# Halved operands for the output product, second pair's weights formed earlier, and the entry's low parts on VectorE, in one hybrid decoder layer

## The chip, the cores and the metric

The kernel runs on 1 core of one Trainium2 chip. The metric is the device time of one launch in microseconds (us), the median of several runs. All times below are in us unless ns is written. Engines are called as the profile calls them: PE (TensorE, matrix products), ACT (ScalarE), DVE (VectorE), POOL (GpSimd), SP (SyncE, which issues every DMA of this kernel).

## What is computed

One layer (DEPTH is 1) of a decoder with parallel branches, for 1024 prompt positions and 8 x 4 sample positions with the same weights. The kernel puts both side by side: 1056 columns of tokens, features on the 128 partitions.

```
h = RMSNorm(x);  p = h @ w_in
A = retention -> GroupNorm -> swish gate;  B = spatial gating unit;  C = cross-attention
x = x + (sig(gA)*A@w_br_ret + sig(gB)*B@w_br_sg + sig(gC)*C@w_br_x) @ w_o      # D = 1024
z = RMSNorm(x) @ w_up                                                          # 2 x 2816 columns
zc = conv_b + sum(conv_w[j] * z shifted by j)                                  # causal, width 3
a, b = split(zc);  x = x + (gelu(a) * b) @ w_down;  y = RMSNorm_final(x)
```

The change touches the second half of this: the product with w_o ("wo" in the code), the norm behind it, the first two of the 22 pairs of columns of w_up, and the entry of the product with w_down.

## The kernel before

**Every fp32 product is three products.** An operand is split into a high part (ACT copies it into the type fp32r) and a low part (value minus high part, one subtraction on DVE or POOL). PE then adds high*high, high*low and low*high in PSUM. So a product needs two elementwise instructions ahead of it for each operand, weights too. `split` makes both parts, `x_split` makes the high part and, if it is given an engine (`vtt` is DVE, `ptt` is POOL), the low part; `x_low` makes a low part alone.

**Order.** The whole kernel is a schedule written out by hand: each engine runs its instructions in the order of the program. Work that belongs beside a product is put in one of two ways: generators in `gens`, of which `hook()` takes a step after every k step of a product at a rate that is set for each stage; and the list `todo` (L1486), of which `do()` takes one entry after every k step of the first products of w_up. An entry's place in the list sets the order in the queues, not a time: an engine runs ahead until something it needs is missing.

**Buffers.** `slot` gives one of 40 buffers of 128 x 1056 (NSLOT); an instruction that writes a new tile waits until the buffer's last reader is done. Weights pass through two raw buffers (`wr`) and three pairs of split buffers (`wh`, `wl`). PSUM holds two accumulators of three banks (`mp`) up to w_o and three of two banks (`bp`) in the products with w_up.

**The stages around the change.** First the branch product "br" (m = 0..7): `mops` gets, for each m, the high and low part of the merged branches over all 1056 columns, the low part on POOL. Then the product with w_o, in two token halves of 528 columns (`half`), each m = 0..7 with eight k steps of six matmuls; behind each m DVE adds the product to the residual (`x2c`), ACT squares, DVE sums the squares, and the half is written to DRAM (`scx`). Beside the second half runs `half_norm` (L1260): the norm of the first half (`norm_sums`, `norm_root`), then for each k the scaling on DVE (`h_scale`, L1257) and the split into the operands B11 and B21, low parts on POOL.

**The first pair of w_up** (the "entry", L1507) is a plain product: two rows r (columns j and 22 + j) times two token halves, each a sum of s = 0, 1. Beside it `todo` norms and scales the second half (A), forms its low parts (L) into B12 and B22, and then the sums and differences t1 to t4 and the splits T2, T3, T1, T4.

**The other 21 pairs** use a 2 x 2 scheme with seven products in place of eight: B11, B21, B22, T2, T3, T1, T4 each times one block of the weights or a sum of blocks. `f_dma` loads a pair's raw weights, `f_sums` forms s1 to s4, `f_prep0` to `f_prep3` split a11|a12, s2|s3, s1|s4 and a22. The products' results are put together with additions that read PSUM (`put`, `put_t`, `z_put`), mostly on DVE. Beside pair j DVE runs the convolution of pair j - 1 (`Conv.first` on ACT, `tap` twice for each of a and b on DVE, `gelu` on ACT, `conv_end` on DVE). Pair 1 is written out (L1539 to 1572), pairs 2 to 21 are the loop at L1593.

**The entry of w_down** is prepared in the last pair by `first_down` (L1574), five steps: loads and splits of the first activations (`a_load`, `a_split`) and weights (`w_dma`, `w_prep`), and the loads of the residual (`x2_load`, eight DMAs from `scx` into `x2t`) in its fourth and fifth step. In `down` DVE adds each finished product to `x2t[m]`; `last_conv` runs beside it.

## Time and profile before

| | us |
|---|---|
| median of 3 runs | 1964.17 (1964.1 to 1965.32) |
| the profiled execution: its time | 1969.01 |
| the profiled execution: its span | 1967.2 |
| PE busy in the span | 1885.8 (96%) |
| DVE, POOL, ACT busy | 1071.7, 963.2, 615.6 |
| mean granted TensorE clock | 0.984 of full speed |
| product "br" ends, product with w_o ends | 1100.5, 1197.9 |
| entry, pair 1, pair 2, pairs 3 to 21 begin | 1199.0, 1230.2, 1260.9, 1291.2 |
| product with w_down begins | 1679.7 |

The last three rows are the starts of matmuls in the timeline of PE, counted from the start of the span. "Busy" is the share of time in which an instruction was under way on an engine; a matmul's end is modelled and matmuls overlap, so the count of matmuls in a stretch says more than the busy time. A row of the chain of waits names an engine, a line of the kernel, and what released it. Nearly all subtractions and sums have L112 (DVE), L115 (POOL) or L118 (DVE, with a scalar), and all matmuls L106, since helpers record them; the tiles' names tell them apart: `mgl` is a low part of `mops`, `xh`/`xl` are the parts of B11 to T4, `wh`/`wl`, `fh`/`fl`, `f` and `fs` are split weights and their sums, `x2c` the residual and the scaled rows, `t` the buffers of t2, `ns`/`nst` the norm, `c` the convolution, `zt`/`zu`/`z`/`zs` results put together, `x` the tiles of `x2t`.

### The profile page before, as it was taken

To read this page: it belongs to the slowest core of one execution; us is meant where nothing else is said; L and a number is where in the kernel's file an instruction comes from. 1 tells how busy PE (TensorE), PEld (TensorE's weight loads), DVE (VectorE), ACT (ScalarE), POOL (GpSimd) and SP (SyncE) were. 2 spreads that over 40 slices of the span, in tenths; PEclk is the share of its full clock that TensorE was granted. 3 is DMA by queue.
4 is the path that set the end of the run, shared out by engine and by line. 5 is a ranking of instruction groups with operands and counts; after the bars stand their busy time and mean duration, and the time that the engine had idled before them with its cause. 6 is when DMAs were issued, how large, how long until landed. Compare 5 with 4: busy or idle time off the path is not lost.

```text
span 1967.2 us, 31365 instructions
## 1 busy us (share of the span) xinstructions
PE 1885.8 (96%) x13201; PEld 1856.8 (94%) x13201; DVE 1071.7 (54%) x1480; ACT 615.6 (31%) x954; POOL 963.2 (49%) x594
## 2 busy tenths in 40 slices
PE   6999999999989999999999999899999999899997
PEld 6999998999989999999999998799999999799996
DVE  8463636453464531111112266699999999644446
ACT  5232232322224332111131233534434344321204
POOL 6242433231644424334254456777777777653404
PEclk9999999999999999999999999899999999899998
DMA  4112131324133313111221532122222223632202
GB/s 182 54 44 90 44 102 37 127 65 152 54 131 108 98 30 146 42 45 48 88 93 43 184 130 76 44 66 88 76 79 77 74 88 99 251 124 105 75 1 89
DMA packets 51740, 174.50 MB, mean 89 GB/s; under 512 B 5712, under 2 KB 8944, under 8 KB 51600
## 3 DMA queue, kind: packets, MB, share of 16 engines
q1 hardware_dynamic: 51600, 172.50, 26.3%
q8 instruction: 104, 1.70, 0.3%
q14 instruction: 36, 0.29, 0.1%
HBM read 137.04 MB, written 35.43 MB: 88 GB/s over the span
## 4 chain that ended last, share of the span: by engine, by line
PE 77%; DVE 9%; issue 5%; ACT 3%; POOL 3%; DMA 2%; SPq 0%; DVEq 0%; POOLq 0%; ACTq 0%
PE mp L106 53%; PE bp L106 19%; PE ap L106 4%; DVE c L118 1%; POOL wl L115 1%; POOL mgl L115 1%; DVE hl L118 1%; DVE s L112 1%; ACT sw L476 1%; DMA xr<-in_xT 1%; DVE x2c L118 1%; DMA scr<-ox 0%; POOL xl L115 0%; DVE rt L118 0%; DVE st L526 0%
## 5 line engine op out<-in xcount | busy, mean ns | idle before, releaser
L115 POOL TENSOR_TENSOR wl<-wr,wh 128x1024 fp32r<-128x1024 f32 x115 | 296.5, 2581 | 425.5 <-ACT wh L150 378.4
L106 PE MATMUL mp<-hh,wh 128*128 128x384 f32 (+1 forms) x1152 | 263.6, 337 | 10.2 <-ACT hh L109 5.3
L106 PE MATMUL mp<-hl,wh 128*128 128x384 f32 (+1 forms) x1152 | 253.8, 328 | 5.0 <-DVE hl L118 5.0
L106 PE MATMUL mp<-hh,wl 128*128 128x384 f32 (+1 forms) x1152 | 251.1, 325 | 0.0
L106 PE MATMUL bp<-xl,wh 128*128 128x264 f32 (+2 forms) x1056 | 217.3, 288 | 6.1 <-POOL xl L115 5.7
L106 PE MATMUL bp<-xh,wh 128*128 128x264 f32 (+2 forms) x1056 | 216.5, 286 | 6.1 <-DVE zu L112 3.5
L106 PE MATMUL bp<-xh,wl 128*128 128x264 f32 (+2 forms) x1056 | 216.3, 286 | 2.1 <-POOL wl L115 2.1
L106 PEld LDWEIGHTS mp<-hh,wh 128*128 128x128 f32 x1152 | 192.2, 191 | 13.2 <-ACT hh L109 5.5
L106 PEld LDWEIGHTS mp<-hl,wh 128*128 128x128 f32 x1152 | 193.3, 190 | 7.5 <-DVE hl L118 7.5
L106 PEld LDWEIGHTS mp<-hh,wl 128*128 128x128 f32 x1152 | 193.3, 190 | 0.0
L112 DVE TENSOR_TENSOR x<-x,mp 128x288 f32<-128x288 f32 (+3 forms) x167 | 105.7, 675 | 128.1 <-PE mp L106 119.2
L106 PEld LDWEIGHTS bp<-xl,wh 128*128 128x128 f32 x1056 | 166.6, 191 | 8.3 <-POOL xl L115 7.3
L106 PEld LDWEIGHTS bp<-xh,wh 128*128 128x128 f32 x1056 | 166.7, 191 | 7.2 <-issue 5.1
L106 PEld LDWEIGHTS bp<-xh,wl 128*128 128x128 f32 x1056 | 166.8, 191 | 2.5 <-POOL wl L115 2.5
L115 POOL TENSOR_TENSOR wl<-fs,wh 128x1024 fp32r<-128x1024 f32 x41 | 123.8, 3020 | 51.4 <-ACT wh L1285 51.3
L118 DVE SCALAR_TENSOR_TENSOR c<-z,hist,c 128x1024 f32<-128x1024 f32 x88 | 134.2, 1526 | 17.8 <-ACT c L109 17.8
L106 PE MATMUL mp<-ach,whs 128*128 128x384 f32 (+3 forms) x524 | 125.1, 328 | 9.2 <-DVE x L112 8.3
L150 ACT CAST wh<-wr 128x1024 fp32r<-128x1024 f32 x100 | 103.9, 1041 | 75.6 <-PE mp L106 50.0
L106 PE MATMUL mp<-acl,whs 128*128 128x384 f32 (+3 forms) x524 | 124.9, 328 | 0.0
L106 PE MATMUL mp<-ach,wls 128*128 128x384 f32 (+3 forms) x524 | 124.8, 328 | 0.0
L112 DVE TENSOR_TENSOR th<-mp,rst 128x768 f32<-128x768 f32 (+1 forms) x48 | 31.7, 701 | 170.9 <-PE mp L106 150.3
L118 DVE SCALAR_TENSOR_TENSOR th<-th,mp 128x768 f32<-128x768 f32 (+1 forms) x48 | 31.7, 701 | 145.4 <-PE mp L106 145.4
(352 smaller groups left out, 4132.7 us busy)
## 6 DMA issues: line engine op xcount, KB each, us to landing
wr<-in_wslab SPq DMA_DIRECT2D x164, 512.0 KB, 3.6
sca<-c SPq DMA_DIRECT2D x22, 528.0 KB, 3.0
opr<-sca SPq DMA_DIRECT2D x22, 528.0 KB, 4.5
opr<-scr SPq DMA_DIRECT2D x16, 528.0 KB, 5.4
scr<-ort SPq DMA_DIRECT2D x8, 528.0 KB, 7.6
x2c<-in_xT SPq DMA_DIRECT2D x8, 528.0 KB, 7.6
scx<-x2c SPq DMA_DIRECT2D x16, 264.0 KB, 2.9
x<-scx SPq DMA_DIRECT2D x8, 528.0 KB, 9.6
```

The source lines that it names most:

```text
L106: nc.tensor.matmul(out=out, lhsT=l, rhs=r, start=start, stop=stop)
L112: nc.vector.tensor_tensor(out=out, in0=a, in1=b, op=op)
L115: nc.gpsimd.tensor_tensor(out=out, in0=a, in1=b, op=op)
L118: nc.vector.scalar_tensor_tensor(out=out, in0=a, scalar=s, in1=b, op0=op0, op1=op1)
L150: nc.scalar.copy(out=hi, in_=raw)
L476: nc.scalar.copy(out=o[a:a + 64], in_=i[b:b + 64])
```

## The change

Five edits in one function.

1. `mops` holds, for each half of the tokens, a list of eight tiles with the high part in the first 528 columns and the low part in the next 528. ACT and POOL run two instructions of 528 columns for each m in place of one of 1056. The product with w_o reads the tiles of its half.
2. The second pair's raw weights (`raw1`) are loaded into buffers of their own behind m = 5 of the first half; a11|a12, the four sums (all on DVE), a22 and s2|s3 are formed in `early1` behind m = 1, 2, 4 and 5 of the second half. s1|s4 and the loads of pair 2 come at the second entry of `todo`. Pair 2's weights are formed earlier in pair 1: a11|a12 behind its first product, the sums behind its third, all on POOL, s2|s3 behind the fourth, s1|s4 behind the fifth.
3. Low parts: in `half_norm` on DVE, one k behind the high part; all eight L, and T1, T3 and T4, on DVE (before: four L on DVE and four on POOL; T1, T3, T4 on POOL). The list `todo` is written anew.
4. In the entry's second half both rows use an operand before the next: (s 0, row 0), (s 0, row 1), (s 1, row 0), (s 1, row 1).
5. `x2_load` moves from the fourth and fifth step of `first_down` to the first and second.

```diff
                 gens.append(late())
             tha.append(gate(("ga", m), 0, m))
         drain()
-        mops = []
+        mops = [[], []]
         for m in range(8):
             ps = fm(("br", m), aops)
             gated(tha[m], ps)
             vtt(acc[m], acc[m], tha[m], ALU.add)
-            mops.append(split(acc[m], "mg"))
+
+            for half in range(2):
+                t = slot("mg", F32R)
+                src = acc[m][:, half * HW:(half + 1) * HW]
+                nc.scalar.copy(out=t[:, 0:HW], in_=src)
+                ptt(t[:, HW:2 * HW], src, f(t)[:, 0:HW], ALU.subtract)
+                mops[half].append(t)
 
 
         x2c = []
...
 
         def half_norm():
 
+            low = lambda k: x_low(("B11", "B21")[k // 4], k % 4, hs(k, 0), vtt)
             norm_sums(0)
             yield
             norm_root(0)
             for k in range(8):
                 h_scale(k, 0)
-                x_split(("B11", "B21")[k // 4], k % 4, hs(k, 0), ptt)
+                x_split(("B11", "B21")[k // 4], k % 4, hs(k, 0), None)
+                if k:
+                    low(k - 1)
                 yield
+            low(7)
 
 
         fraw, fw = {}, {}
...
 
         fsum = {}
 
-        def f_sums(j, sub):
+        def f_sums(j, sub, sub34=ptt):
 
             a11, a12, a21, a22 = f_quads(j)
             fsum[j] = (slot("fs"), slot("fs"))
             s2, s3, s1, s4 = [t[:, 512 * i:512 * i + 512] for t in fsum[j] for i in range(2)]
             sub(s1, a21, a22, ALU.add)
             sub(s2, s1, a11, ALU.subtract)
-            return lambda: (ptt(s3, a11, a21, ALU.subtract), ptt(s4, a12, s2, ALU.subtract))
-
-        def f_prep0(j):
+            return lambda: (sub34(s3, a11, a21, ALU.subtract), sub34(s4, a12, s2, ALU.subtract))
+
+        def f_prep0(j, own=False):
             fw[j] = {}
-            f_parts(j, ("a11", "a12"), fraw[j][0])
+            f_parts(j, ("a11", "a12"), fraw[j][0], own)
 
         def f_prep1(j, own=False):
             f_parts(j, ("s2", "s3"), fsum[j][0][:, 0:1024], own)
...
             ptt(t[:, 512:1024], a22, f(t)[:, 0:512], ALU.subtract)
             fw[j]["a22"] = (t[:, 0:512], t[:, 512:1024])
             del fraw[j]
-            f_dma(j + 1)
+            if j > 1:
+                f_dma(j + 1)
+
+
+        def raw1():
+            fraw[1] = [slot("fr", shape=[P, 1024]) for _ in range(2)]
+            for t, key in zip(fraw[1], (("up", 1), ("up", NFF + 1))):
+                dma(t, wslab[SLABS.index(key)])
+
+        early1 = [int, lambda: f_prep0(1, True), lambda: f_sums(1, vtt, vtt)(), int, lambda: f_prep3(1),
+                  lambda: f_prep1(1, True), int, int]
 
         for half in range(2):
             rate[0] = 0.25
...
                 lv = lo.rearrange("p (k c) -> p k c", c=P)
                 ps = mp()
                 for k in range(8):
-                    rh, rl = mops[k]
+                    rh, rl = mops[half][k][:, 0:HW], mops[half][k][:, HW:2 * HW]
                     for i, (a, r) in enumerate(((hv, rh), (hv, rl), (lv, rh))):
                         for q in range(2):
-                            c0 = half * HW + q * QW
+                            c0 = q * QW
                             mm(ps[:, q, 0:QW], a[:, k, :], r[:, c0:c0 + QW], start=(k == 0 and i == 0),
                                stop=(k == 7 and i == 2))
                     if k == 0 or k == 3:
                         w_ahead()
-                        if wst["p"] == FAST0 and 1 not in fraw:
-                            f_dma(1)
                     hook()
                 w_free(key)
                 o = quarters(hs(m, half))
...
                     act(sq[:, 0:HW], hs(m, half), AF.Square)
                     vtt(s, s, sq[:, 0:HW], ALU.add)
                 dma(scx[m][:, half * HW:(half + 1) * HW], hs(m, half))
+                if half:
+                    early1[m]()
+                elif m == 5:
+                    raw1()
             drain()
             if half == 0:
                 gens.append(half_norm())
...
             o = tt2[k // 2][:, (k % 2) * HW:(k % 2 + 1) * HW]
             vtt(h(k + 4, 0), h(k + 4, 0), o, ALU.subtract)
 
-        T1s = lambda k: x_split("T1", k, h(k, 0), ptt)
-        T3s = lambda k: x_split("T3", k, h(k, 1), ptt)
-        T4s = lambda k: x_split("T4", k, h(k + 4, 0), ptt)
+        T1s = lambda k: x_split("T1", k, h(k, 0), vtt)
+        T3s = lambda k: x_split("T3", k, h(k, 1), vtt)
+        T4s = lambda k: x_split("T4", k, h(k + 4, 0), vtt)
         todo = deque([
-            lambda: (norm_sums(1), f_sums(1, ptt)()), lambda: f_prep0(1), None, None, None, None, lambda: norm_root(1),
-            None, lambda: A(0), lambda: (A(1), L(0, vtt), L(1, ptt)), lambda: A(2), lambda: (A(3), L(2, vtt), L(3, ptt)),
-            lambda: A(4), lambda: (A(5), L(4, vtt), L(5, ptt)), lambda: A(6), lambda: (A(7), L(6, vtt), L(7, ptt)),
-            None, lambda: f_prep2(1, True), None, lambda: (t1(0), t1(1)), lambda: (t1(2), t1(3)), None,
-            lambda: (t2(0), t2(1)), lambda: (t2(2), t2(3)), None, lambda: f_prep1(1), lambda: (t2l(0), t2l(1)),
-            lambda: (t2l(2), t2l(3), f_prep3(1)), lambda: (t4(0), t4(1)), lambda: (t4(2), t4(3)), None, None,
-            lambda: (t3(0), t3(1)), lambda: (T3s(0), T3s(1)), lambda: (T1s(0), T1s(1)), lambda: (t3(2), t3(3)), None,
-            lambda: (T3s(2), T3s(3)), None, lambda: (T1s(2), T1s(3)), None, None, None, lambda: T4s(0), None,
-            lambda: T4s(1), None, lambda: T4s(2), None, lambda: T4s(3)])
+            lambda: norm_sums(1), lambda: (f_prep2(1), f_dma(2)), None, None, None, lambda: norm_root(1), lambda: A(0), lambda: (A(1), L(0, vtt)),
+            lambda: (A(2), L(1, vtt)), lambda: (A(3), L(2, vtt)), lambda: (A(4), L(3, vtt)), lambda: (A(5), L(4, vtt)),
+            lambda: (A(6), L(5, vtt)), lambda: (A(7), L(6, vtt)), lambda: L(7, vtt), None,
+            lambda: (t1(0), t1(1)), lambda: (t1(2), t1(3)), lambda: (t2(0), t2(1)), lambda: (t2(2), t2(3)), None,
+            lambda: (t2l(0), t2l(1)), lambda: (t2l(2), t2l(3)), None, lambda: (t3(0), t3(1)), lambda: (t3(2), t3(3)),
+            None, None, lambda: (t4(0), t4(1)), None, lambda: (t4(2), t4(3)), None,
+            None, None, None, lambda: (T3s(0), T3s(1)), None, None, None, None,
+            lambda: (T3s(2), T3s(3)), lambda: (T1s(0), T1s(1)), None, lambda: (T1s(2), T1s(3)), lambda: T4s(0),
+            lambda: T4s(1), lambda: T4s(2), lambda: T4s(3)])
 
         def do():
             ticks()
...
         z0 = [z_new(0), z_new(NFF)]
         wab = [w_get(("up", 0)), w_get(("up", NFF))]
         conv = [Conv(0, *z0[0]), Conv(NFF, *z0[1])]
-        for n, (r, half) in enumerate([(0, 0), (1, 0), (0, 1), (1, 1)]):
-            ps = None
-            for s in range(2):
-                ps = prod([x[:, 512 * s:512 * s + 512] for x in wab[r]], f"B{s + 1}{half + 1}", ps, s == 0, s == 1, do)
-            z_put(ps, half, *z0[r])
-            if n > 1:
-                w_free(("up", NFF * r))
+        for half in range(2):
+            pss = [None, None]
+
+            for s, r in ((0, 0), (1, 0), (0, 1), (1, 1)) if half == 0 else ((0, 0), (0, 1), (1, 0), (1, 1)):
+                pss[r] = prod([x[:, 512 * s:512 * s + 512] for x in wab[r]], f"B{s + 1}{half + 1}", pss[r], s == 0, s == 1,
+                              do)
+                if s:
+                    z_put(pss[r], half, *z0[r])
+                    if half:
+                        w_free(("up", NFF * r))
         rate[0] = 0.0
         x2t = []
         oraw = {}
...
         d = fw.pop(1)
         p1, r, u3, u4 = blocks(1)
         put(prod(d["a11"], "B11", tick=do), p1)
+        f_prep0(2)
         n = prod(d["a12"], "B21", tick=do)
         za = z_new(1)
         z_put(n, 0, *za, p1)
         n = prod(d["s4"], "B22", tick=do)
         z_put(n, 1, *za)
+        f_sums(2, ptt)()
         put(prod(d["s2"], "T2", tick=do), r, p1)
+        f_prep1(2)
         pa.first()
         pa.tap(1)
         put(prod(d["s3"], "T3", tick=do), u3, r)
-        f_prep0(2)
         pa.tap(0)
         pa.gelu()
+        f_prep2(2)
         n = prod(d["s1"], "T1", tick=do)
         assert not todo
         put_t(n, u4, r)
...
         z_put(n, 1, *zb, u3)
         vtt(za[0][:, 2 + HW:2 + TP], za[0][:, 2 + HW:2 + TP], u4[:, 0:2 * HA], ALU.add)
         vtt(za[1][:, :, 2:6], za[1][:, :, 2:6], by4(u4[:, 2 * HA:HW]), ALU.add)
-        s34 = f_sums(2, vtt)
-        s34()
-        f_prep1(2)
         pb.first()
         pb.tap(1)
-        f_prep2(2)
         conv = [Conv(1, *za), Conv(NFF + 1, *zb)]
         n = prod(d["a22"], "T4", tick=do)
         z_put(n, 0, *zb, u3)
...
             a_load(1)
             w_dma()
             w_dma()
+            x2_load(range(4))
             yield
             a_split(0)
             w_prep()
+            x2_load(range(4, 8))
             yield
             a_split(1)
             w_prep()
             yield
             a_load(2)
             a_load(3)
-            x2_load(range(4))
-            yield
-            x2_load(range(4, 8))
+            yield
             yield
 
         for j in range(2, NFF):
```

## The prediction

> **What bounds the kernel now.** I read the page first, then the busy times by stretch around the stages that the diff touches, then who makes PE wait, then the timelines of DVE and POOL there.
>
> ```profile
> PE 1885.8 (96%) x13201; PEld 1856.8 (94%) x13201; DVE 1071.7 (54%) x1480; ACT 615.6 (31%) x954; POOL 963.2 (49%) x594
> ```
> ```profile
> 1211.40:1230.20 18.80, 15.19 (x97) 13.61 (x98) 18.78 (x20) 8.37 (x14) 9.76 (x5) 0.91 0.05 19
> 1230.20:1260.90 30.70, 23.46 (x170) 22.22 (x169) 15.66 (x18) 15.14 (x29) 26.52 (x18) 0.92 0.06 18
> 1260.90:1291.20 30.30, 25.57 (x168) 24.55 (x169) 27.88 (x35) 12.18 (x20) 19.33 (x14) 0.86 0.18 62
> ...
> 1311.60:1332.00 20.40, 20.40 (x171) 20.40 (x170) 19.27 (x21) 8.50 (x15) 15.22 (x11) 1.00 0.24 79
> ...
> 1679.70:1713.00 33.30, 25.00 (x125) 24.24 (x126) 21.77 (x21) 11.70 (x16) 19.53 (x7) 0.85 0.77 288
> 1713.00:1736.00 23.00, 23.00 (x144) 23.00 (x144) 10.55 (x16) 6.29 (x7) 17.01 (x8) 1.00 0.61 211
> ```
> ```profile
> PE mp L106 <- DVE x L112: 8.3, 3, 4.2
> ...
> PE bp L106 <- POOL xl L115: 5.9, 7, 2.8
> PE bp L106 <- DVE zu L112: 5.5, 2, 3.5
> ...
> PE mp L106 <- POOL mgl L115: 1.0, 1, 1.0
> ```
>
> The columns of the stretches are length, then busy time and count of PE, its weight loads, DVE, ACT and POOL, then granted clock. PE bounds the kernel, and no matmul is added or removed, so the change can win only what PE loses. A pair costs 20.4 where nothing disturbs it (1311.6 to 1332). A pair has 168 matmuls, so the 96 of the entry's second half should cost 96 x 20.4/168 = 11.7; they take 18.8. Pair 1 takes 30.7, pair 2 30.3, each some 10 over. The first 125 matmuls with w_down should cost 125 x 23.0/144 = 20.0 and take 33.3. With the single wait for `mgl` (1.0) that is 7.1 + 10.3 + 9.9 + 13.3 + 1.0 = 41.6 to be had at most. In pair 1 DVE is busy 15.7 of 30.7 and POOL 26.5; in pair 2 it is DVE, 27.9 of 30.3.
>
> **Part 1, the halves of `mops`.**
>
> ```profile
> L115 POOL TENSOR_TENSOR mgl<-th,mgh x8: 2439/2468/2486, 1023.4 to 1104.7; 128x1056 fp32r<-128x1056 f32 x8
> ```
> ```profile
> L115 POOL TENSOR_TENSOR xl<-x2c,xh x24: 1296/1334/1883, 1159.8 to 1255.3; 128x528 fp32r<-128x528 f32 x24
> ...
> L112 DVE TENSOR_TENSOR xl<-x2c,xh x4: 695/697/709, 1212.1 to 1221.2; 128x528 fp32r<-128x528 f32 x4
> ```
>
> A low part of 528 columns costs POOL 1.33 in place of 2.47 for 1056. The first half of m = 7 is there 1.14 sooner, its copy sooner too, so the wait of 1.0 goes. The two instructions cost POOL 0.2 more for each m, beside products of 72 matmuls, 72 x 23.0/144 = 11.5. **-1.0.**
>
> **Part 2, the entry.** Its norm is late because POOL forms pair 1's sums beside it.
>
> ```profile
> 1205.84 1.19 DVE L118 SCALAR_TENSOR_TENSOR nst<-rst 128x528 f32<-128x528 f32 x1
> 1207.06 2.78 DVE L112 TENSOR_TENSOR nst<-nst 128x528 f32<-128x528 f32 x1
> ...
> 1210.62 1.45 DVE L118 SCALAR_TENSOR_TENSOR x2c<-x2c,vecs,rst 128x528 f32<-128x528 f32 x2
> 1212.08 0.71 DVE L112 TENSOR_TENSOR xl<-x2c,xh 128x528 fp32r<-128x528 f32 x1
> ...
> 1232.55 2.55 DVE L112 TENSOR_TENSOR x2c<-x2c,t 128x528 f32<-128x528 f32 x4
> 1235.02 2.56 DVE L112 TENSOR_TENSOR x2c<-x2c 128x528 f32<-128x528 f32 x4
> ```
> ```profile
> 1232.41 7.42 POOL L115 TENSOR_TENSOR wl<-fs,wh 128x1024 fp32r<-128x1024 f32 x1 [5.92 <-ACT wh L1285]
> ...
> 1256.55 2.35 POOL L115 TENSOR_TENSOR wl<-wr,wh 128x1024 fp32r<-128x1024 f32 x1
> ...
> 1262.33 1.29 POOL L115 TENSOR_TENSOR fs<-wr 128x512 f32<-128x512 f32 x1
> ```
>
> The two norm steps took 1.19 and 2.78 with POOL at work; their like take 0.71. POOL keeps only s1|s4 there (2.35, over before the norm's matmul), so 0.5 + 2.1 go, and the root comes one tick (0.7) sooner: the first scaling starts at 1210.6 - 3.3 = 1207.3. From then on DVE works alone: a scaling costs 0.7 from start to start, a subtraction 0.62 (four in 2.47, 1232.55 to 1235.02). Low part k is ready at 1207.3 + 0.7(k+2) + 0.62(k+1): 1213.3 for k = 3, 1217.9 for k = 7, where no scaling is left. PE starts the half at 1211.4 and wants k = 3 at 1213.8. With rows sharing operands it wants k = 4 only after two products, 1217.2, and k = 7 at 1219.7, so nothing waits; in the old order k = 7 would be wanted at 1216.8, 1.1 too soon. The half takes 11.7 in place of 18.8: **-7.1**, to 1223.1. If POOL were not done, half of it would stay: bound -3.5.
>
> Ahead of this, in the second half of w_o, DVE gets eight low parts and four sums (12 x 0.62 = 7.4), and POOL loses eight low parts (10.7) and gets 2.35 + 1.29 + 2.35 = 6.0 of weights. Both have what they need an evacuation or a slab ahead, in products of 48 matmuls (48 x 20.4/168 = 5.8) with two accumulators, so I cost this at nothing; uncovered, it would cost at most what is net added to DVE and POOL together, 2.7. On SP `raw1` stands behind a write already due and ahead of the next slab, two issues of 0.4.
>
> **Part 3, pair 1.** Twelve low parts move from POOL (12 x 1.33 = 16.0) to DVE (12 x 0.62 = 7.4), and POOL now forms pair 2's four sums (5.2) and three low parts there. DVE's chain from 1207.3: scalings and L 10.6, t1 to t4 with T2's low parts 20 x 0.62 = 12.4, T3, T1, T4 7.4, two results (1.2): 1238.9. PE, starting at 1223.1, wants T3 at 1234.8, T1 at 1237.7, T4 at 1240.6: all in time. What is late next is new: `f_prep1(2)` stands on ACT ahead of pair 0's first convolution step, and waits for three POOL sums behind a low part, 2.35 + 3 x 1.29 = 6.2. Queued behind it: that step, DVE's tap, and DVE's `put` of s3, whose accumulator pair 2's first product wants at 1243.5. How does POOL fare beside a dense DVE? The row at 1232.41 says badly: 7.42 in place of 2.35; it got through at 1239.8, so its own 2.35 began only at 1237.5, when the eight DVE instructions from 1232.55 were over. So I let POOL start at 1238.9: + 6.2 + ACT's copy 1.0 + step 1.2 + tap 1.4 + result 0.6 = 1249.3. If POOL goes between instead, DVE ends its two results at 1238.9 + 6.2 + 1.3 = 1246.4, the last product follows (2.9), again 1249.3. Pair 1 takes 26.2 in place of 30.7: **-4.5**. With full overlap it would end at 1243.5, -10.3.
>
> The Trainium skill, "SBUF — State Buffer", section "Who interferes with whom", says that a DVE instruction with two SBUF inputs and a GpSimd instruction that reads SBUF exclude each other for a whole instruction, and that the one that starts first goes first. The 2.78 agrees; the 7.42 does not, since eight DVE instructions that started later went ahead of it. By that rule the second of the two orders above would hold, and the sum would be the same 1249.3.
>
> **Part 4, pair 2.**
>
> ```profile
> 1260.68 1.27 DVE L118 SCALAR_TENSOR_TENSOR c<-z,hist,c 128x1024 f32<-128x1024 f32 x1
> ...
> 1262.04 0.76 DVE L112 TENSOR_TENSOR zu<-bp,zt 128x496 f32<-128x496 f32 x2
> ...
> 1264.18 0.68 DVE L112 TENSOR_TENSOR fs<-wr 128x512 f32<-128x512 f32 x1
> ...
> 1275.10 1.26 DVE L112 TENSOR_TENSOR c<-c 128x1056 f32<-128x1056 f32 x1
> ...
> 1293.08 1.28 DVE L118 SCALAR_TENSOR_TENSOR c<-z,hist,c 128x1024 f32<-128x1024 f32 x1 [0.73 <-ACT c L109]
> ...
> 1298.58 1.74 DVE L118 SCALAR_TENSOR_TENSOR c<-z,hist,c 128x1024 f32<-128x1024 f32 x1
> ```
> ```profile
> L118 DVE SCALAR_TENSOR_TENSOR c<-zs,hist,c 128x32 f32<-128x32 f32 x4 | 5.3, 1322 | 0.0
> ```
> ```profile
> 1250.19 0.65 PE L106 MATMUL bp<-xl,fh 128*128 128x248 f32 x2
> 1250.64 0.65 PE L106 MATMUL bp<-xh,fl 128*128 128x248 f32 x2
> ```
>
> Its weights are ready now (before, `wh` and `wl` came late). DVE is not: of pair 1's work it has left, at 1249.3, three taps of 1.36 (1260.68 to 1262.04), results of 2.1 (1262.04 to 1264.18) and 0.6, and 1.2 for the gated product: 8.0, to 1257.3. POOL's two low parts (4.7) lengthen this by between nothing and 4.7. In the undisturbed pair (1311.6 to 1332) the four short taps took 5.3 in place of 4 x 0.24, so 4.3 went to 15.2 of POOL: 0.28 for one, hence 1.3, DVE free at 1258.6. That is 9.3 behind pair 2's start; in pair 3 it was 1.9 (1291.2 to 1293.08). Of these 7.4, 4.3 are slack, as s2's result was read 7.4 after that start and its accumulator is wanted at 4 x 2.9 = 11.7. So PE waits 3.1 (6.5 at the other end), and after a wait matmuls run at half rate for a while: 0.45 for two in place of 0.24, for seven such rows behind 1249, 1.4. Pair 2 takes 24.9: **-5.4**. Pairs 3 on: DVE has 1.1 spare in each, so nothing.
>
> **Part 5, the residual.**
>
> ```profile
> 1681.22 6.15 SPq L103 DMA_DIRECT2D x<-scx x8
> ```
> ```profile
> 1688.45 1.32 DVE L112 TENSOR_TENSOR x<-x,mp 128x768 f32<-128x768 f32 x2 [8.90 <-DMA x<-scx]
> ...
> 1696.81 2.62 DVE L118 SCALAR_TENSOR_TENSOR c<-z,hist,c 128x1024 f32<-128x1024 f32 x1
> ...
> 1701.67 1.30 DVE L112 TENSOR_TENSOR x<-x,mp 128x768 f32<-128x768 f32 x2
> 1702.90 2.28 DVE L118 SCALAR_TENSOR_TENSOR c<-z,hist,c 128x1024 f32<-128x1024 f32 x1
> ...
> 1707.39 1.30 DVE L112 TENSOR_TENSOR x<-x,mp 128x768 f32<-128x768 f32 x2
> 1708.62 2.24 DVE L112 TENSOR_TENSOR c<-c 128x1056 f32<-128x1056 f32 x1
> 1710.78 1.30 DVE L112 TENSOR_TENSOR x<-x,mp 128x768 f32<-128x768 f32 x2
> ```
>
> The loads are issued at 1681.2, behind four weight loads; DVE stands 8.9 for the first one with the last convolution queued behind it. Moved, they pass two weight loads and a write on SP (eight issues, 6.2 at most) and need eight buffers sooner; operands that the last pair has finished with give them. Then DVE starts when the first product ends, 1679.7 + 2.9 = 1682.6, and until the sixth addition has six of 1.23, two taps of 1.36, two slowed ones (4.9 to 1701.67, 4.5 to 1707.39) and 2.2: 21.7, to 1704.3, against 1712.0. The eighth product waits for that. -7.7, less 1.4 for half rate: **-6.3**. Bounds: nothing, if the buffers come as late as the loads did; -12.1 if the taps are not slowed and PE is not held (1699.9).
>
> **Sum.** 1.0 + 7.1 + 4.5 + 5.4 + 6.3 = 24.3 off the profiled execution's 1969.0 (span 1967.2), which is 4.8 over the median of the runs; taken off that, 1964.2 - 24.3 = 1940.
>
> **Rivals.** *DVE takes POOL's place in full.* All of POOL's work in pair 1 (2.35 + 4 x 1.29 + 4.7 = 12.2) is added to DVE's, and there is no slack: 1207.3 + 10.6 + 12.4 + 7.4 + 1.2 + 2.0 + 8.0 + 12.2 = 1261.1, and a pair of 19.3 more ends at 1280.4, where my sum has 1249.3 + 24.9 = 1274.2: 1946. For it: pair 2 is already 27.9 of 30.3 on DVE. Against: half of pair 1 DVE stands idle. *The loads come no sooner,* since buffers are the limit: 1946; with the rival above 1953. *The engines overlap almost wholly:* another 5 in pair 1, 4 in pair 2, 2 at w_down: 1929. *Slower: DVE never catches up.* It enters pair 3 late, and each late pair meets POOL's 2.4 at more places. A pair has 1.1 spare; one more such block in each of 19 pairs costs 1.3 x 19 = 24, which eats the whole gain, and two cost 3.7 x 19 = 70: 2010. It decides from one block a pair. Against: pair 2 was DVE's in this trace too, and the pairs after it run free.
>
> **How the numbers follow.** Forecast, with its bounds 1931 to 1944: 0.60. DVE in full or loads no sooner, 1944 to 1954: 0.22. Near-total overlap: 0.09. Faster parts all lost, within 0.2% (3.9 us, about what a measurement of this kernel can tell from no change): 0.04. Slower: 0.05. So faster 0.91, same 0.04, slower 0.05, and the range 1931 to 1954.
>
> **What would show it.** Right: no wait for `mgl`; 96 matmuls of the entry's second half in about 12; POOL no longer named for `xl`; pair 2 starting 26 after pair 1 with a wait behind DVE's `zu` or the convolution; `x` loads issued before 1675 and no DMA wait on DVE at w_down. Wrong: waits in the second half of w_o, PE short of full in pairs 3 to 21, or w_down's first products waiting for buffers.

## The result and the profile after

The changed kernel takes 1949.34 us (median of 4 runs, 1946.45 to 1949.61), the kernel before in the same session 1964.74 (1964.1 to 1966.55). The ratio is 0.9917, 95% interval 0.99 to 0.9934: faster by 15.4 us. The forecast was 1940 in a range of 1931 to 1954. The profiled executions took 1969.01 before and 1949.1 after (span 1947.3); they differ by 19.9, since the profiled execution of before lay 4.3 above its median and that of after at its own. (Of one kernel of the experiments, mix_order, the profiled execution took 6489 us at a granted clock of 0.27; it is left out below, so that kernel has a time and no stages.)

The page of the changed kernel, busy time of the engines:

```profile
PE 1878.4 (96%) x13201; PEld 1852.8 (95%) x13201; DVE 1078.1 (55%) x1506; ACT 615.9 (32%) x962; POOL 927.7 (48%) x576
```

As many matmuls as before, and PE bounds both kernels. POOL lost 35.5 of busy time and DVE gained 6.4. To see where the time went, the stages are laid side by side. The table is worked out from the starts of matmuls in the timelines of PE, by their number, which is the same in both kernels; the first row counts from PE's first matmul (4.8 to 5.0 behind the start of the span), the last one to the start of PE's last.

| stage, us | before | after | difference | forecast |
|---|---|---|---|---|
| ahead of the output product | 1095.63 | 1096.62 | +1.0 | 0 |
| product with w_o, first half | 48.19 | 46.75 | -1.4 | -1.0 |
| product with w_o, second half | 50.19 | 53.65 | +3.5 | 0 |
| entry | 31.19 | 23.99 | -7.2 | -7.1 |
| pair 1 | 30.73 | 30.17 | -0.6 | -4.5 |
| pair 2 | 30.30 | 22.37 | -7.9 | -5.4 |
| pairs 3 to 21 | 388.49 | 389.49 | +1.0 | 0 |
| first 144 matmuls with w_down | 36.54 | 28.41 | -8.1 | -6.3 |
| rest | 240.67 | 241.13 | +0.5 | 0 |

Two rows are off by much: the second half of the product with w_o, and how the gain divides between pairs 1 and 2. The busy times by stretch for the changed kernel, with columns as before (length; PE, its weight loads, DVE, ACT, POOL; granted clock; DMA), from the second half with w_o to pair 3 and then the beginning of w_down:

```profile
1148.20:1201.86 53.66, 48.17 (x391) 47.41 (x389) 41.70 (x42) 22.68 (x32) 26.99 (x11) 1.00 0.33 110
...
1214.08:1225.85 11.77, 11.77 (x98) 11.77 (x97) 11.69 (x19) 5.23 (x9) 0.00 (x0) 1.00 0.00 1
1225.85:1256.02 30.17, 23.24 (x170) 23.03 (x169) 29.77 (x38) 17.01 (x31) 14.97 (x9) 0.84 0.06 18
1256.02:1278.40 22.38, 21.10 (x170) 20.70 (x169) 21.31 (x25) 8.93 (x17) 14.58 (x12) 0.99 0.17 61
1278.40:1298.94 20.54, 20.54 (x168) 20.54 (x169) 19.66 (x23) 8.67 (x15) 16.05 (x11) 1.00 0.27 88
1667.90:1696.30 28.40, 25.34 (x145) 24.85 (x145) 22.38 (x23) 11.65 (x15) 19.66 (x8) 0.94 0.66 230
```

The entry's second half is free of waits (11.77 for the length and for PE). The two steps of its norm that took 1.19 and 2.78 before take, in DVE's timeline of the changed kernel:

```profile
1208.02 0.70 DVE L118 SCALAR_TENSOR_TENSOR nst<-rst 128x528 f32<-128x528 f32 x1
1208.75 0.71 DVE L112 TENSOR_TENSOR nst<-nst 128x528 f32<-128x528 f32 x1
```

The first scaling starts 8.4 behind the entry's first matmul, 11.6 before, with 8.3 forecast. That agrees with the account of part 2. But no run undoes edit 1, edit 4, the pair's earlier weights or the entry's low parts alone, so what each of them is worth in the first half with w_o and in the entry is not shown.

Pair 1 has changed sides: before, POOL was busy 26.5 of 30.7 and DVE 15.7; now DVE is busy 29.8 of 30.2 and POOL 15.0. Who makes PE wait, of the changed kernel (total, times, longest):

```profile
PE bp L106 <- DVE zt L112: 6.9, 1, 6.9
...
PE mp L106 <- DVE x L112: 3.1, 2, 2.6
PE mp L106 <- DVE x2c L118: 2.8, 1, 2.8
...
PE bp L106 <- DVE zu L112: 1.1, 1, 1.1
```

POOL's `xl` and `mgl` are gone from this list, and the wait for `x` fell from 8.3 to 3.1. Two waits are new: 6.9 for `zt`, the result of s2 in pair 1, and 2.8 for `x2c`, an evacuation in the second half with w_o.

**The 6.9 of pair 1.** POOL's timeline of the changed kernel there (start, duration):

```profile
1231.97 5.02 POOL L115 TENSOR_TENSOR wl<-wr,wh 128x1024 fp32r<-128x1024 f32 x1 [24.72 <-PE bp L106]
...
1238.88 1.69 POOL L115 TENSOR_TENSOR fs<-wr 128x512 f32<-128x512 f32 x1 [1.26 <-DVE xl L112]
1240.65 1.65 POOL L115 TENSOR_TENSOR fs<-fs,wr 128x512 f32<-128x512 f32 x1
1242.27 1.74 POOL L115 TENSOR_TENSOR fs<-wr 128x512 f32<-128x512 f32 x1
1243.97 1.73 POOL L115 TENSOR_TENSOR fs<-wr,fs 128x512 f32<-128x512 f32 x1
1246.79 2.48 POOL L115 TENSOR_TENSOR wl<-fs,wh 128x1024 fp32r<-128x1024 f32 x1 [1.10 <-ACT wh L1295]
```

and DVE's beside it:

```profile
1235.27 14.57 DVE L112 TENSOR_TENSOR xl<-x2c,xh 128x528 fp32r<-128x528 f32 x10
1249.77 0.69 DVE L112 TENSOR_TENSOR zt<-bp,zt 128x528 f32<-128x528 f32 x1
```

Both orders that the prediction weighed occur. The first instruction of POOL (5.02 in place of 2.35) is passed by five instructions of DVE that start behind it and end ahead of it, like the 7.42 of before. The next five, the four sums and the low part of s2|s3, go between DVE's subtractions: ten low parts take 14.57 in place of 6.2. The Trainium skill, "SBUF — State Buffer", section "Who interferes with whom", has the engine that starts first go first for a whole instruction. The five agree with that, the 5.02 does not.

PE's timeline shows what is behind the wait, and the stretch after it what clock it ran at:

```profile
1250.61 0.78 PE L106 MATMUL bp<-xh,f 128*128 128x264 f32 x2 [6.93 <-DVE zt L112]
```
```profile
1250.60:1256.02 5.42, 5.41 (x24) 5.42 (x25) 5.23 (x11) 3.07 (x4) 0.10 (x1) 0.50 0.01 3
```

The last product of the pair, 24 matmuls, runs at a granted clock of 0.50 from end to end: 5.4 in place of 2.9.

**The 2.8 with w_o.** DVE's timeline of the changed kernel in its second half:

```profile
1174.80 0.69 DVE L112 TENSOR_TENSOR fs<-fr 128x512 f32<-128x512 f32 x1
1175.52 2.77 DVE L112 TENSOR_TENSOR fs<-fs,fr 128x512 f32<-128x512 f32 x1
1178.21 0.68 DVE L112 TENSOR_TENSOR fs<-fr 128x512 f32<-128x512 f32 x1
1178.82 0.68 DVE L112 TENSOR_TENSOR fs<-fr,fs 128x512 f32<-128x512 f32 x1
1179.42 0.75 DVE L118 SCALAR_TENSOR_TENSOR x2c<-x2c,vecs,rst 128x528 f32<-128x528 f32 x1
...
1182.02 0.69 DVE L118 SCALAR_TENSOR_TENSOR x2c<-mp,x2c 128x528 f32<-128x528 f32 x1
```

The product of m = 3 was done at 1174.1. Its evacuation (the addition that empties its accumulator), the last row, stands behind the four sums, one of which waits 2.1 for POOL, and behind two scalings and two low parts: it starts 7.9 behind the product, and PE wants the accumulator at 1180.0.

### The profile page after: what moved, and what is told of

Its sections match the earlier page's. It is cut to its first block, busy times and chain, and to the rows that moved or that the text cites. A ratio compares the mean times of both kernels' runs of the same rounds, so it can differ in the third digit from the quotient of the medians.

```text
span 1947.3 us, 31390 instructions
## 1 busy us (share of the span) xinstructions
PE 1878.4 (96%) x13201; PEld 1852.8 (95%) x13201; DVE 1078.1 (55%) x1506; ACT 615.9 (32%) x962; POOL 927.7 (48%) x576
## 4 chain that ended last, share of the span: by engine, by line
PE 80%; DVE 11%; ACT 3%; issue 3%; DMA 1%; POOL 1%; SPq 0%; DVEq 0%; ACTq 0%; POOLq 0%
PE mp L106 55%; PE bp L106 20%; PE ap L106 4%; DVE xl L112 1%; DVE c L118 1%; DVE x2c L118 1%; DVE hl L118 1%; DVE s L112 1%; DMA xr<-in_xT 1%; DMA scr<-ox 0%; ACT sw L476 0%; DVE rt L118 0%; DVE st L526 0%; SPq L103 0%; PE ap L576 0%
## 5 line engine op out<-in xcount | busy, mean ns | idle before, releaser
L106 PE MATMUL bp<-xh,wh 128*128 128x264 f32 (+2 forms) x1040 | 211.4, 284 | 1.0 <-DVE x2c L118 0.9
L106 PE MATMUL bp<-xl,wh 128*128 128x264 f32 (+2 forms) x1040 | 211.1, 284 | 0.0
L106 PE MATMUL bp<-xh,wl 128*128 128x264 f32 (+2 forms) x1040 | 211.0, 284 | 0.0
L106 PEld LDWEIGHTS bp<-xh,wh 128*128 128x128 f32 x1040 | 162.4, 188 | 1.4 <-issue 1.4
L106 PEld LDWEIGHTS bp<-xl,wh 128*128 128x128 f32 x1040 | 162.4, 188 | 0.0
L106 PEld LDWEIGHTS bp<-xh,wl 128*128 128x128 f32 x1040 | 162.3, 188 | 0.0
L115 POOL TENSOR_TENSOR wl<-fs,wh 128x1024 fp32r<-128x1024 f32 x41 | 119.0, 2902 | 55.7 <-ACT wh L1295 55.7
L118 DVE SCALAR_TENSOR_TENSOR c<-z,hist,c 128x1024 f32<-128x1024 f32 x88 | 124.6, 1416 | 4.2 <-ACT c L109 2.5
L112 DVE TENSOR_TENSOR th<-mp,rst 128x768 f32<-128x768 f32 (+1 forms) x48 | 31.6, 701 | 170.9 <-PE mp L106 150.3
```

Of the source, the lines that this page charges most:

```text
L106: nc.tensor.matmul(out=out, lhsT=l, rhs=r, start=start, stop=stop)
L112: nc.vector.tensor_tensor(out=out, in0=a, in1=b, op=op)
L115: nc.gpsimd.tensor_tensor(out=out, in0=a, in1=b, op=op)
L118: nc.vector.scalar_tensor_tensor(out=out, in0=a, scalar=s, in1=b, op0=op0, op1=op1)
```

## The experiments

All kernels are the changed kernel with one edit, unless it says otherwise. Medians are of 4 runs where nothing else stands. A ratio is to the kernel before as it was timed in the same session (medians of 1964.74 to 1966.49). The stages of the profiled executions, by the same matmuls as above:

| kernel | median, us | ratio to before | w_o 2nd half | entry | pair 1 | pair 2 | both | first 144 w_down |
|---|---|---|---|---|---|---|---|---|
| before | 1964.74 | | 50.19 | 31.19 | 30.73 | 30.30 | 61.0 | 36.54 |
| before_again | 1965.59 (one run) | | 50.19 | 30.95 | 30.73 | 30.31 | 61.0 | 34.83 |
| changed | 1949.34 | 0.9917 [0.99, 0.9934] | 53.65 | 23.99 | 30.17 | 22.37 | 52.5 | 28.41 |
| r_late | 1955.87 | 0.9949 [0.9935, 0.9964] | 53.66 | 23.99 | 30.18 | 22.38 | 52.6 | 36.05 |
| sums_m4 | 1947.25 | 0.9902 [0.9887, 0.9917] | 52.03 | 25.22 | 29.24 | 23.33 | 52.6 | 27.34 |
| lows_pool | 1947.07 | 0.9908 [0.9891, 0.9924] | 54.06 | 23.99 | 29.26 | 23.26 | 52.5 | 27.36 |
| weights_late | 1948.04 | 0.9907 [0.9891, 0.9924] | 52.11 | 25.32 | 29.14 | 23.39 | 52.5 | 28.41 |
| t_lows_pool | 1954.93 | 0.9946 [0.9929, 0.9962] | 53.65 | 23.99 | 34.74 | 27.14 | 61.9 | 27.39 |
| w2_back | 1945.34 | 0.9895 [0.9881, 0.991] | 53.66 | 23.99 | 20.58 | 31.61 | 52.2 | 27.34 |
| mix | 1944.27 | 0.989 [0.9875, 0.9905] | 53.66 | 23.99 | 24.55 | 27.21 | 51.8 | 27.38 |
| mix_order | 1943.92 (three runs) | 0.989 [0.9874, 0.9907] | | | | | | |
| s3_first | 1945.83 | 0.9901 [0.9885, 0.9918] | 53.65 | 23.99 | 21.10 | 30.33 | 51.4 | 28.15 |
| mix_late | 1946.5 | 0.99 [0.9885, 0.9915] | 52.09 | 24.36 | 24.57 | 25.96 | 50.5 | 28.42 |
| no_taps | 1945.58 (one run) | | 54.86 | 23.98 | 30.17 | 20.79 | 51.0 | 28.26 |

The first half with w_o took 48.19 in both profiles of before and 46.75 in every other kernel. Where an edit does not reach them, the stages repeat within 0.3, apart from the second half with w_o in no_taps (54.86 for 53.65), the first matmuls with w_down (27.3 to 28.4), pairs 3 to 21 (389.1 to 390.3) and the border of pairs 1 and 2, which moves by 1 with their sum unchanged. The stretch ahead of the change varies from 1093.8 to 1096.8 whatever the kernel; so a median says less here than a stage.

### The residual's loads alone: r_late

```diff
             w_dma()
             w_dma()
-            x2_load(range(4))
             yield
...
             a_load(3)
+            x2_load(range(4))
             yield
+            x2_load(range(4, 8))
             yield
```

> The changed kernel with one part undone: the residual's loads stand in the fourth and fifth step of first_down again. Theory (the loads, and nothing else, gave the 8.1 us that the first 144 matmuls with w_down got shorter by): these go from 28.4 us back to about 36.5, DVE waits about 8 us for the first x again, everything ahead of w_down stays, and the kernel is about 8 us slower than the changed one (near 1957). Rival (DVE comes to w_down with less behind it, since pairs 3 to 21 started better): the first 144 matmuls stay under 32 us and the kernel stays within 3 us of the changed one.

The beginning of w_down goes back to 36.05 and the median up by 6.5; nothing else moves. Who makes PE wait, in this kernel:

```profile
PE mp L106 <- DVE x L112: 8.1, 3, 3.7
```

This is the 8.3 of before. Edit 5 alone is worth 7.6 by the stage.

### What stands ahead of the evacuations: sums_m4, lows_pool, weights_late

In sums_m4 the four sums move from m = 2 to m = 4, and a22 and s2|s3 to one m later:

```diff
-        early1 = [int, lambda: f_prep0(1, True), lambda: f_sums(1, vtt, vtt)(), int, lambda: f_prep3(1),
-                  lambda: f_prep1(1, True), int, int]
+        early1 = [int, lambda: f_prep0(1, True), int, int, lambda: f_sums(1, vtt, vtt)(), lambda: f_prep3(1),
+                  lambda: f_prep1(1, True), int]
```

> The changed kernel with the second pair's four sums on DVE formed behind m = 4 of w_o's second half in place of m = 2, and a22 and s2|s3 one m later. Theory (the sums stand in DVE's queue ahead of the evacuation of m = 3, and that is why PE waits 2.85 us there): no wait for x2c in the second half of w_o, which takes 50.2 us in place of 53.6; the kernel is about 3 us faster than the changed one, near 1946. Rival (the eight low parts on DVE, which meet POOL's weights, are the load, whatever else stands there): a wait of 1 to 3 us stays, and the second half takes over 52 us.

In lows_pool the low parts of `half_norm` go back to POOL:

```diff
-                x_split(("B11", "B21")[k // 4], k % 4, hs(k, 0), None)
-                if k:
-                    low(k - 1)
+                x_split(("B11", "B21")[k // 4], k % 4, hs(k, 0), ptt)
                 yield
-            low(7)
```

> The changed kernel with the eight low parts of half_norm on POOL again (as before the change), the four sums still on DVE behind m = 2. Theory (the sums are the cause of the wait in w_o's second half): a wait for x2c of 1 to 3 us stays, the second half takes over 52 us, and the kernel stays within 2 us of the changed one. Rival (the low parts are the cause): no such wait, 50.2 us, about 3 us faster than the changed one, unless POOL is then late with the weights of the entry.

In weights_late the low parts of a11|a12 move to m = 3 as well, and a22 to m = 5:

```diff
-        early1 = [int, lambda: f_prep0(1, True), lambda: f_sums(1, vtt, vtt)(), int, lambda: f_prep3(1),
-                  lambda: f_prep1(1, True), int, int]
+        early1 = [int, int, int, lambda: f_prep0(1, True), lambda: f_sums(1, vtt, vtt)(),
+                  lambda: (f_prep3(1), f_prep1(1, True)), int, int]
```

> The changed kernel with pair 1's early weights later in the second half of the output product: the low parts of a11|a12 from m = 1 to m = 3, the four sums from m = 2 to m = 4, a22 from m = 4 to m = 5 (the rest of s2|s3 stays at m = 5). Theory (the evacuations of m = 2 and 3 came 5 and 8.5 behind their products since POOL's low part of a11|a12 and the sums stood among eight scalings and low parts): the wait of 2.8 goes and the second half takes 50.2 to 51.5 in place of 53.6; POOL's work comes nearer to the norm and may cost the entry up to 1: kernel 1946 to 1948. Rival (DVE has too much in this half wherever it stands): the wait only moves to m = 5 or 6, the half stays at 53 to 54, the kernel at 1949.

Moving the sums takes 1.6 off the half, but the work that follows them comes nearer to the norm, and the entry gets 1.2 longer: 77.3 for half and entry against 77.6. weights_late is the same trade (77.4; with the same edit in mix_late, further down, the entry paid only 0.4). Some waits for evacuations stay; in sums_m4, at the edge of what its rival expected:

```profile
PE mp L106 <- DVE x2c L118: 1.0, 2, 0.6
```

In lows_pool the half takes 54.06. PE waits there at the same place, 2.0 in place of 2.85, in a row that names ACT's `xh`:

```profile
1179.41 0.70 DVE L118 SCALAR_TENSOR_TENSOR x2c<-mp,x2c 128x528 f32<-128x528 f32 x1
1180.25 0.72 PE L106 MATMUL mp<-mg,wh 128*128 128x264 f32 x4 [2.03 <-ACT xh L1233]
```

But this matmul does not read `xh`, and it starts 0.14 behind the end of DVE's evacuation, as the one of the changed kernel does (1182.71, 1182.85). So it is most likely the same wait, shorter by 0.8, with the four sums still ahead of the evacuation (1171.16 to 1178.13). The half is not shorter all the same, since PE went on at about half rate: a granted clock of 0.60 in the next 3.2, and 7.45 for the next product where the changed kernel's took 6.16. The last section shows that such a drop need not come from the edit.

So the place of the sums is about half of the loss, as moving them showed, and the low parts on DVE have a smaller share; none of the three kernels brings the half back to 50.2. What stays are short waits for later evacuations (1.0 in all in sums_m4, 1.3 in weights_late), and which of DVE's instructions ahead of them cause them stays open.

### Pair 2's weights, and the low parts: w2_back, t_lows_pool

In w2_back pair 2's weights are formed where the kernel before formed them:

```diff
-        f_prep0(2)
         n = prod(d["a12"], "B21", tick=do)
...
-        f_sums(2, ptt)()
         put(prod(d["s2"], "T2", tick=do), r, p1)
-        f_prep1(2)
...
         put(prod(d["s3"], "T3", tick=do), u3, r)
+        f_prep0(2)
...
-        f_prep2(2)
...
+        s34 = f_sums(2, vtt)
+        s34()
+        f_prep1(2)
         pb.first()
         pb.tap(1)
+        f_prep2(2)
```

> The changed kernel with the third pair's weights formed where they were before the change (a11|a12 behind the fifth product of pair 1, sums and the rest behind the sixth, s1 and s2 on DVE). Theory (in pair 1 it is POOL's work on these weights, going between DVE's subtractions, that makes the result of s2 late, so that PE waits 6.9 us): no POOL work stands beside the low parts of T3, T1 and T4, these end some 7 us sooner, the wait before the last product falls under 2 us, and pair 1 takes about 23 us in place of 30.2; pair 2 then waits for its weights and takes 26 to 30 us in place of 22.4. The sum of both is 49 to 53 us against 52.5, so the kernel is within 3 us of the changed one. Rival (the twelve low parts on DVE are too much by themselves): pair 1 stays at 28 us or more and the sum of both rises to 57 us or more.

Pair 1 runs at full speed, 20.58. DVE's timeline of w2_back, the low parts and the result of s2 as above:

```profile
1236.13 6.26 DVE L112 TENSOR_TENSOR xl<-x2c,xh 128x528 fp32r<-128x528 f32 x10
1242.32 0.70 DVE L112 TENSOR_TENSOR zt<-bp,zt 128x528 f32<-128x528 f32 x1
```

The ten low parts take 6.26 with POOL away and 14.57 with POOL's work on pair 2's weights between them. That was pair 1's loss, shown. But pair 2 now takes 31.6, and both together 52.2: forming the weights sooner has only moved the loss from one pair to the other.

In t_lows_pool the other half of the edit is undone: T1, T3 and T4 get their low parts from POOL again (`vtt` to `ptt` in `T1s`, `T3s`, `T4s`).

> The changed kernel with the twelve low parts of T1, T3 and T4 formed on POOL again, as before; pair 2's weights stay beside pair 1, on POOL too. Theory (POOL has little of pair 1 to itself, so what stands on it ends late): POOL has 12 x 1.33 + 3 x 2.4 + 4 x 1.3 = 28.4 in pair 1, so T4's last low part is ready some 5 to 7 later than DVE made it; pair 1 takes 35 to 37 in place of 30.2, with waits for POOL xl, pair 2 stays at 22 to 24, and the kernel at 1954 to 1957. Rival (what held pair 1 was that DVE had too much): DVE is 7.4 shorter, pair 1 takes some 25 and the kernel 1944.

Both pairs take 61.9, as before the change (61.0). The busy times of pairs 1 and 2 in t_lows_pool:

```profile
1223.50:1258.24 34.74, 24.50 (x171) 22.81 (x169) 13.18 (x19) 14.71 (x28) 28.55 (x20) 0.90 0.05 16
1258.24:1285.38 27.14, 24.22 (x169) 23.59 (x169) 25.18 (x34) 11.84 (x20) 15.56 (x12) 0.88 0.18 61
```

POOL is busy 28.6 of 34.7 while DVE stands idle for 21.6. The theory had pair 1 nearly right (34.7, with 35 to 37 expected) and pair 2 not: 27.1 for 22 to 24. So all that the change wins in these two pairs is won by the twelve low parts on DVE, and the earlier weights of pair 2 win nothing.

### Can both pairs be had? mix, mix_order, s3_first, no_taps, mix_late

In mix the sums of pair 2 go to DVE, behind its last low part:

```diff
-        f_sums(2, ptt)()
         put(prod(d["s2"], "T2", tick=do), r, p1)
-        f_prep1(2)
+        f_sums(2, vtt, vtt)()
         pa.first()
+        f_prep1(2)
         pa.tap(1)
```

> The changed kernel with one move: pair 2's four sums are formed on DVE, behind its result of s2 and so behind the last low part of T4, in place of on POOL beside them; ACT copies them behind the first step of the convolution and not ahead of it; the low parts of a11|a12 stay where the change put them. Theory (pair 1 was lost because POOL's sums went between DVE's subtractions): pair 1 takes 21 as it did with the weights back; the sums end 2.5 after the result of s2, a copy of 1.0 and a low part of 2.4 follow, 2 behind the point where PE wants s2's weights, with some half rate: pair 2 takes 23 to 25. Both together 44 to 46 in place of 52.5, the kernel at 1941 to 1944. Rival (the work of pairs 1 and 2 on DVE and POOL sets their sum, however it is ordered: 52.5 and 52.2 in the two orders so far): the sum stays at 51 to 53 and the kernel at 1947 to 1950.

The kernel's time came out as the theory expected, 1944.27, but not for its reason: both pairs take 51.8, which is the rival's number. The mechanism of pair 1 is borne out once more. With only the low part of a11|a12 left on POOL beside them, DVE's ten low parts take:

```profile
1233.78 7.87 DVE L112 TENSOR_TENSOR xl<-x2c,xh 128x528 fp32r<-128x528 f32 x10
```

The edit's own gain is 0.8. The rest of the median's 5 us is, by the profiled executions, in stretches that the edit does not touch (ahead 1094.4 against 1096.6, w_down 27.4 against 28.4). In mix_order pair 2's product a12 comes ahead of s2:

```diff
+            if j == 2:
+                n = prod(d["a12"], "B21")
...
+                put(prod(d["s2"], "T2"), r, p1)
+                ticks()
```

> The kernel of mix, with pair 2's products a11, a12, s2 in that order in place of a11, s2, a12, so that the weights of s2 are wanted a product (2.9) later. Theory: the wait of 2 that mix should have for them goes, pair 2 takes 21 to 23, both pairs 42 to 44, the kernel 1939 to 1942. Rival (the sum of the work): as mix, with the wait at another place, 1947 to 1950; or, if DVE's convolutions are late next, as mix within 1.

1943.78 to 1945.37: as mix. Waits of PE longer than 1 in both pairs of mix, from its timeline of PE:

```profile
1248.90 0.81 PE L106 MATMUL bp<-xh,wh 128*128 128x264 f32 x2 [3.34 <-DVE zu L112]
...
1271.56 0.51 PE L106 MATMUL bp<-xh,f 128*128 128x264 f32 x2 [2.09 <-DVE zu L112]
```

No wait for the weights of s2 is among them, so there was none to remove. The first is for the result of s3, which stands on DVE behind a tap of pair 0's convolution. In s3_first that result goes ahead of the tap:

```diff
         f_prep1(2)
-        pa.tap(1)
         put(prod(d["s3"], "T3", tick=do), u3, r)
+        pa.tap(1)
         pa.tap(0)
...
-        f_prep2(2)
...
+        f_prep2(2)
...
-        pb.tap(1)
         conv = [Conv(1, *za), Conv(NFF + 1, *zb)]
...
         z_put(n, 0, *zb, u3)
+        pb.tap(1)
         pb.tap(0)
```

> The kernel of mix with the result of s3 on DVE ahead of the first tap of pair 0's convolution (in mix behind it, 3.6 later, where pair 2's first product waited 3.3 for that accumulator), the second part's first tap behind the last result, and the low parts of s1|s4 behind the result of s1. Theory (order: a result stood behind a tap that POOL held up): pair 1 takes 21 to 22 in place of 24.6, pair 2 stays at 25 to 27.2, both together 47 to 49, the kernel at 1940 to 1942. Rival (amount: from pair 1's last low part to the middle of pair 2 DVE has no gap, so its convolutions come out at the same time in any order): pair 1 gets the same 21 to 22, but pair 2 gives it back, 29 to 30, together 51 to 52, the kernel at 1944.

Pair 1 takes 21.10 and pair 2 gives it all back, 30.33: the rival's numbers. Pairs 1 and 2 in s3_first:

```profile
1225.37:1246.47 21.10, 20.78 (x171) 20.50 (x169) 21.07 (x33) 13.64 (x28) 5.71 (x4) 1.00 0.01 2
1246.47:1276.80 30.33, 24.30 (x170) 23.70 (x170) 29.05 (x36) 12.84 (x21) 18.95 (x13) 0.89 0.21 72
```

and in mix:

```profile
1224.35:1248.90 24.55, 20.90 (x170) 20.50 (x168) 24.52 (x35) 14.82 (x28) 8.42 (x4) 0.99 0.08 23
1248.90:1276.12 27.22, 24.18 (x169) 23.55 (x170) 25.25 (x34) 11.85 (x20) 15.58 (x12) 0.88 0.18 61
```

In DVE's column (behind PE and its weight loads) it is busy 50.1 of 51.4 and 49.8 of 51.8. It has hardly a gap to give (its busy time includes what POOL slows it by), and in these orders of its work only the pair that shows the loss changes. In no_taps the changed kernel's work on DVE is made less: the four taps of pair 0's convolution are left out, so that the kernel computes something else.

```diff
-        pa.tap(1)
...
-        pa.tap(0)
...
-        pb.tap(1)
...
-        pb.tap(0)
```

> The changed kernel without the four taps of pair 0's convolution (two steps of the filter are left out, 1.36 each on DVE where nothing disturbs them, 5.4 in all), nothing else changed. In three orders of the same work pairs 1 and 2 together took 52.5, 52.2 and 51.8. Theory (DVE is the bound of the two pairs taken together, its instructions follow one another with no gap): both together get shorter by 5.4 or more, up to 10 since two of the short taps stood 2.3 each for POOL: 43 to 47, and the kernel at 1939 to 1944. Rival (the bound is the chain from POOL's sums through ACT to PE, or the half rate behind its waits): the pairs stay at 50 to 52.5, the kernel at 1946 to 1949.

Pair 2 falls to 20.8, close to its floor of 20.4, but pair 1 stays at 30.17, and both win 1.6 and not 5.4. The theory fails in the form given: DVE's work is not one pool for both pairs. The taps stand behind the result of s2, and pair 1 ends by what stands ahead of it, which is the ten low parts with POOL between them. In the changed kernel the bound of pair 1 is therefore that chain. That in mix and s3_first it is DVE's whole queue is argued from the busy times alone; no run leaves the taps out there. Why the sums of the pairs lie within 1.1 of each other in all these orders (51.4 to 52.5) is not shown.

In mix_late the edits of mix and weights_late stand together.

> The kernel of mix together with that of weights_late. Theory: both gains add, 1944.3 less 2 to 3: 1941 to 1943. Rival: nothing gained in the second half, 1944 to 1945.

1946.5 is above both expectations: by the median the gains do not add. Pairs 1 and 2 take 50.5, the least of all, and half and entry 76.5 in place of 77.6, but pairs 3 to 21 take 390.2 (389.3 in mix) and w_down 28.4 (27.4 in mix). Its runs lie 4.3 apart, and the profiled one was the fastest of them (1943.68).

The lowest medians are those of mix and mix_order, which cannot be told apart. The four runs of mix, 1943.79 to 1944.84, lie below all four of the changed kernel, but those of w2_back (1943.06 to 1947.39) lie on both sides of them. mix and the changed kernel were not timed side by side, their intervals against the kernel before, 0.9875 to 0.9905 and 0.99 to 0.9934, overlap a little, and only 0.8 of the difference is in stages that the edit reaches.

### The kernel before once more: before_again

> The kernel before, unchanged, profiled once more: the profiled execution of it that the prediction started from lay 4.3 above the median of its runs, that of the changed kernel at its median. If that lies in stretches that the change does not touch (the one ahead of the output product, the pairs from 3 on), the stages keep 50.2, 31.2, 30.7, 30.3 and 36.6 within 0.5 each. If one of these stages was a slow draw, it comes out 2 or more lower here, and what the change gained there is less by as much.

Every stage that the change reaches repeats within 0.3, but one: the beginning of w_down took 34.83 and not 36.54. So the profile that the prediction was worked from had a w_down that was 1.7 worse than in the next one. The two executions differ by 3.4; of the rest, 1.0 lies ahead of the change, 0.7 behind the first 144 matmuls with w_down and 0.2 in the entry, less 0.5 by which PE's first matmul starts later in the second.

## Why the prediction held, point by point

**The total.** The range held, but not where the forecast stood in it: 1949.34 is above the forecast's own bounds (1931 to 1944) and among the times that were given to DVE taking POOL's place in full or to loads that come no sooner (1944 to 1954), and neither of these is what happened. The sum of 24.3 stands against 21.8 in the stages that it names. That it comes so near is in part luck: 3.5 in the second half with w_o and 3.9 in pair 1 were missed one way, and 2.5 in pair 2, 1.8 at w_down and 0.5 in parts 1 and 2 the other. The other 6.8 of the miss (1940 against 1949.3) is not in the steps: the sum was taken from one execution and subtracted from the median of others. From profile to profile it gave 1944.7 where 1949.1 came. Beside the 2.5 in the stages, 1.9 of that is in stretches that the change does not touch, above all 1.0 ahead and 0.05 in each of the 19 pairs that run free in both kernels (median 20.43 for 20.38).

**Part 1** held: the wait for `mgl` is gone, -1.4 for -1.0.

**Part 2** held for the entry, -7.2 for -7.1: the norm's steps are short, and the half runs its 96 matmuls without a wait; which of the edits that meet there gives how much is open. Its other claim failed: "Both have what they need an evacuation or a slab ahead, in products of 48 matmuls (48 x 20.4/168 = 5.8) with two accumulators, so I cost this at nothing; uncovered, it would cost at most what is net added to DVE and POOL together, 2.7." It cost 3.5, outside the bound. Counting what an engine has to do in a stretch misses what an instruction costs while it queues: the sums came as one block of 4.7 between two evacuations, on top of low parts that stood while POOL worked (2.6 and 2.9 for 0.7). "Wrong: waits in the second half of w_o" was named as a sign, and came.

**Part 3** is the step that failed, -0.6 for -4.5. The mechanism is the one that the text gave for its second order, POOL going between, and w2_back shows it alone. Two terms of it were too small. "If POOL goes between instead, DVE ends its two results at 1238.9 + 6.2 + 1.3 = 1246.4" is 23.3 behind pair 1's start; the first of them alone ended 24.6 behind. The low parts lost 8.3 to POOL (14.57 less 6.26) and not 6.2, as the low part of s2|s3 (2.48 at 1246.79) went ahead of a subtraction too. And "the last product follows (2.9)" took 5.4, since a wait of 6.9 stands ahead of it and the half rate that part 4 counted for its own wait was not counted for this one. 1.3 + 2.5 is nearly all of the difference of 4.0.

**Part 4** came out better, -7.9 for -5.4: DVE took taps off its list during that slow last product, so PE waits 1.1 for `zu` where 3.1 was forecast, with hardly any half rate (clock 0.99). The two errors partly cancel, which nothing in the text foresaw: -8.5 for both pairs where -9.9 was forecast. That the pairs' gain is the low parts' and not the earlier weights' the prediction did not see; t_lows_pool and w2_back showed it.

**Part 5** held with a size that was too small, -8.1 for -6.3 (7.6 by r_late, 6.4 against the second profile of before). Its own step is near: the sixth addition was to end 24.6 behind the first product's start, and in the changed kernel's timeline of DVE it ends 24.2 behind 1667.9:

```profile
1688.66 2.25 DVE L112 TENSOR_TENSOR c<-c 128x1056 f32<-128x1056 f32 x1
1690.83 1.30 DVE L112 TENSOR_TENSOR x<-x,mp 128x768 f32<-128x768 f32 x2
```

The loads are issued from 1654.1 on, so the buffers were there.

**The rivals.** That DVE takes POOL's place in full had the right engine (29.8 of 30.2 in pair 1) and too high a price: it gave pairs 1 and 2 57.3 (1280.4 less 1223.1), the forecast 51.1, and they took 52.5. Loads that come no sooner are refuted by w_down's 28.4, which r_late undoes. Near-total overlap is refuted by the ten low parts. That DVE never catches up is refuted by pairs 3 to 21, 20.43 at the median.

## What to carry to other kernels

Before work is moved from a late engine to an idle one, add up what the receiving engine has to do until the result that ends the stage, with the prices it pays while the first engine still runs beside it: ten subtractions cost 6.3 alone and 14.6 with five of POOL's instructions between them. Where DVE was busy in nearly all of two stages, forming weights sooner only chose the stage that showed the loss. Taking work off an engine helps where it stands ahead of the result that ends the stage: of the 5.4 that no_taps took off DVE behind that result, 1.6 was won. Work the sum out of a profile stage by stage, but profile the kernel twice before taking that sum off a median, since one stage of it may be an unlucky draw (here 1.7).
